# A carried block's cast and low placed further behind its transfers, and two columns of an output product computed as a pair with two quads

## The chip, the cores and the metric

The kernel runs on one core of a Trainium2 chip. The metric is the device time of one execution in microseconds (us), as a median of several. The engines are named as in the profile: PE is TensorE's matmuls and PEld its weight loads, DVE is VectorE, ACT is ScalarE, POOL is GpSimd, SP is SyncE, which here only issues transfers.

## The reference

One layer with a sequence of 256 tokens and a width of 2048, all in fp32: a feed-forward part, a mixer and a second feed-forward part, each with a norm before and after it and added to what came in.

```python
f = _swiglu(_rmsnorm(h, ln_ffn1_pre[l]), ffn1_gate[l], ffn1_up[l], ffn1_down[l])
h = h + MACARON_WEIGHT * _rmsnorm(f, ln_ffn1_post[l])
mx = _hybrid_mixer(_rmsnorm(h, ln_mix_pre[l]), w_in[l], ..., w_out[l])
h = h + _rmsnorm(mx, ln_mix_post[l])
f = _swiglu(_rmsnorm(h, ln_ffn2_pre[l]), ffn2_gate[l], ffn2_up[l], ffn2_down[l])
h = h + MACARON_WEIGHT * _rmsnorm(f, ln_ffn2_post[l])
```

`_swiglu` is `(silu(x @ w_gate) * (x @ w_up)) @ w_down` with 5632 inner columns. The mixer computes a recurrent branch and a pooling branch, gates and adds them to `m`, and returns `m @ w_out`, with `w_out` 2048 x 2048. The change touches the two feed-forward parts and this last product.

## The kernel before, in words

**Products.** Each fp32 operand is split in two: `wH` is the weight rounded by a cast on ACT (L151), `wL` the rest, a subtraction on DVE (L152). One product is three matmuls, wH·xH, wL·xH and wH·xL (`mm3`, L175 to L177), each over 512 weight columns. Weights come in pairs of two k rows by 512 columns: one transfer of 512 KB issued by SP (L137) into one of four `w32` buffers, one cast, one low, into one of five buffers each for `wH` and `wL`. A k row is multiplied with both halves of the tokens (128 each), so a pair takes 12 matmuls.

**Pairs of columns and quads.** `seven` (L321) does two column blocks together, f then l: first f's pairs, then l's. A few k pairs are done as quads instead (`quad`, L358): two k rows of both columns at once, with 7 products for 8, in the manner of Strassen. A quad needs sums of weights on DVE (`t13` L374, the halves of `t24` L378 and L382), casts (L389) and lows (L390) of weights and sums, and sums of activations made ahead (`sums`, L254: L265 to L277 on DVE, high parts on ACT L310, lows L314). It takes 21 matmuls in place of 24 and collects into the banks p1, p5, p6 and p7 ("ms" in the profile) besides the columns' own banks ("mm"). Behind the last quad comes `merge` (L406): ACT copies p1 into a buffer `u` (L411), DVE adds p6, p7, p5 and p5, then f's two own banks (L414); then f's result is evaluated. Adding l's banks (`total`, L423) comes at the end.

**Feed-forward.** Its 5632 inner columns are eleven blocks of 512, b = 0 to 10, each a gate (f) and an up column block (l). Blocks 2 to 10 use `seven` with three quads (`NG`, `SPOTS`), so ten pairs and three quads, 183 matmuls. The third quad comes behind the second pair of l's part; then three pairs follow, beside which the merge runs. There are four "mm" banks, two of f and two of l, so the next block's first matmul needs a bank that the merge has read.

**The carried block.** A block's result is multiplied, transposed 32 by 32 on DVE (L589) and then carried into the next block (`carry_at`, L591): 8 us after that block's start POOL issues sixteen transfers `x<-T` (L601) that complete the transpose. For each token half h follow the cast on ACT (`high`, L613) at `CARRY[h]` behind the transfers' issue and the low on DVE (`low`, L617) 2 us after it. The result is a part of `hT`, which only the down product reads. That product (`post`, L726) has 44 k rows and two column pairs, with seven and eight quads; the last 16 k rows of its last column are done by token halves (`by_half`, `TRAIL`), so that the norm and the next transposes of the first half run beside the second.

**The output product** `m @ w_out` is the same `post` with 16 k rows: four column blocks, each by `gemm_tok` (L179) with eight pairs, the last by halves.

**What sets the order.** The order of instructions on PE, ACT and DVE is written out ahead by a plan of times: `put` (L128) queues matmuls, each with its time (0.2265 us per matmul), `at` (L101) places an event at a time of this plan, and `slot` (L106) gives the planned time at which a weight buffer comes free. `run` (L112) writes the instructions in that order; nothing reorders them on the chip. POOL's and SP's instructions follow in the order in which they were written.

Of the kernel before, what the change touches and what calls it, by code (L numbers as in the profile page):

```python
# [22 lines left out]
NKD = D // P  # L23
NKF = DFF // P
# [17 lines left out]
TRAIL = 16  # L42
# [1 line left out]
TURNS = [[4.2, 5.3, 6.4, 7.5], [5.3, 6.0, 6.7, 7.4]]  # L44
WARM = 12
TB = 4
NQ = {False: 7, True: 8}
QUADS = {False: ((8, 12), (0, 3, 5, 7, 9)), True: ((2, 4, 6, 8, 10, 12), (1, 3))}
FAST = range(2, 11)
CARRY = (10, 13)  # L50
NG, SPOTS = 3, ((2, 4), (1,))

ROWS = [("ln_mix_pre", 16), ("ln_ffn2_pre", 16), ("mu", 26), ("w0", 8), ("a0", 8),
# [4 lines left out]
class Block:  # L58
# [259 lines left out]
                                                  else (third, fourth))):  # L318
            s.at(when + 1.7 * i, fn)

    def seven(s, wf, cf, wl, cl, at, KT, T, sm, n, spots, ev_first, ev_last, trail=False,  # L321
              one_end=False):


# [79 lines left out]
        u = []  # L404

        def merge():  # L406
            m = s.clk

            def start():
                u.extend(s.tmp("u") for _ in range(4))  # L410
                nc.scalar.copy(u[0], bank["p1"])  # L411

            def add(o, b, i):
                V.tensor_tensor(out=u[o], in0=bank[b], in1=u[i], op=ALU.add)  # L414
            s.at(m + 0.2, start)
            for j, a in enumerate(((1, "p6", 0), (2, "p7", 1), (1, "p5", 1), (3, "p5", 2),
                                   (1, "f0", 1), (3, "f1", 3))):
                s.at(m + 0.7 + 0.1 * j, lambda a=a: add(*a))
            s.at(m + 4, lambda: ev_first(0, u[1]))
            s.at(m + 4.6, lambda: ev_first(1, u[3]))  # L420

        def total(h):
            V.tensor_tensor(out=u[2 * h], in0=bank[f"l{h}"], in1=u[2 * h], op=ALU.add)  # L423
# [5 lines left out]
        def both():  # L429
            total(0)  # L430
            total(1)
            ev_last((u[0], u[2]))
        q = 0
        stop = KT - (TRAIL if trail else 0)
        for part, w, c0, b in ((0, wf, cf, "f"), (1, wl, cl, "l")):
            for i, k in enumerate(range(K0, stop if part else KT, 2)):
                pair(k, w, c0, b)
                if i in spots[part]:
                    quad(q)
                    q += 1  # L440
                    if q == n:
                        merge()
        if trail:
            s.by_half(wl, cl, stop, KT, s.clk, AHEAD[0],
                      lambda k, h: mul(f"l{h}", rows(k, h), ws[k]), keep, finish)
# [145 lines left out]
    def carry_at(s, T1, T, t):  # L591
# [28 lines left out]
        for h in range(2):  # L620
            s.at(t + CARRY[h], lambda h=h: high(h))
            s.at(t + CARRY[h] + 2, lambda h=h: low(h))

# [3 lines left out]
    def ffn(s, wg, wu, wd, uT, rs, gpost, resid, emit, reload, xs=None):  # L627
        nc = s.nc
        hT, sm = [], []
        at = s.T_at(uT)  # L630
        nb = NKF // 4

        st = {}

        def block(b):
            sig = [None, None]
            T1 = []

            def turned(h, src):
                if not T1:  # L640
                    T1.append(s.unit(p="T1"))
                s.turn(T1[0], h, src)

            def ev_g(h, ps):
                sig[h] = s.tmp("sg")
                nc.scalar.activation(out=sig[h], in_=ps, func=AF.Silu, scale=r[h])

            def ev_f(h, u):
                sig[h] = u
                nc.scalar.activation(out=u, in_=u, func=AF.Silu)  # L650

            def ev_l(o):
                for h in range(2):
                    nc.vector.tensor_tensor(out=o[h], in0=o[h], in1=sig[h], op=ALU.mult)
                for h in range(2):
                    turned(h, o[h])

            def ev_um(h, ps):
                nc.vector.scalar_tensor_tensor(out=sig[h], in0=ps, scalar=r[h], in1=sig[h],
                                               op0=ALU.mult, op1=ALU.mult)  # L660
                turned(h, sig[h])

            r = rs if b < 2 else [1.0, 1.0]
            if b > 0:
                s.carry_at(*st["T1"], s.clk + 8)
            st["T1"] = (T1, hT)
            if b == 0:
                s.gemm_tok(wg, 0, at, NKD, ev_g, lead=True, xs=xs)
                s.gemm_tok(wu, 0, at, NKD, ev_um, hold=True)
                while s.after:  # L670
                    s.after.pop(0)()
                st["rb"] = s.rtmp("rsb")
                s.spread(rs, st["rb"])
                return
            if b == 1:
                st["nT"], st["su"] = s.normed(uT, st["rb"], s.clk + 4), []
                s.sums(st["nT"], st["su"], s.clk + 16)
                s.sums(st["nT"], st["su"], s.clk + 27, nq=1)
            nT, su = st["nT"], st["su"]
            if b in FAST:  # L680
                s.seven(wg, b * 512, wu, b * 512, s.T_at(nT), NKD, nT, su, NG, SPOTS,
                        ev_f, ev_l, one_end=True)
                return
            x = at if b == 1 else s.T_at(nT)
            s.gemm_at(wg, b * 512, x, NKD, ev_g)
            s.gemm_at(wu, b * 512, x, NKD, ev_um)

        for b in range(nb):
            block(b)
        s.carry_at(*st["T1"], s.clk + 8)  # L690
        s.post(wd, s.T_at(hT), NKF, gpost, 0.5, resid, emit, reload, hT, sm)

    def spread(s, rs, out):

# [28 lines left out]
            s.at(t + 9.5 * i, lambda i=i: one(i))  # L723
        return nT

    def post(s, wd, at, KT, gpost, fac, resid, emit, reload, hT=None, sm=None):  # L726
        nc = s.nc
        gb = [s.unit(p="gb") for _ in range(2)]
        fg = [[s.unit(p="fg") for _ in range(2)] for _ in range(2)]
        ss = [s.small(4, "ss") for _ in range(2)]  # L730

        def cc_(u, c):
            return u[c // 2][:, (c % 2) * 512:(c % 2) * 512 + 512]

        part = [None, None]
        kf = 1.0 / (D * fac ** 2)

        late = 0.7 if hT is not None else 0.0

        def ev_of(c):  # L740
            def ev(h, ps):
                if h == 0 and c % 2 == 0:
                    nc.gpsimd.dma_start(out=gb[c // 2], in_=gpost[c * 512:c * 512 + 1024]
                                        .partition_broadcast(P))
                def scale():
                    nc.vector.tensor_tensor(out=cc_(fg[h], c), in0=ps, in1=cc_(gb, c),
                                            op=ALU.mult)
                s.sumsq(ps, ss[h][:, c:c + 1])
                if c < 3:
                    scale()  # L750
                if c == 2 and h == 0:
                    reload()
                if c == 2:
                    p = s.small(1, "rt", bufs=2)
                    nc.vector.tensor_reduce(out=p, in_=ss[h][:, :3], axis=AX.X, op=ALU.add)
                    part[h] = s.small(1, "rp", bufs=2)
                    nc.vector.tensor_scalar(out=part[h], in0=p, scalar1=kf,
                                            scalar2=NORM_EPS / fac ** 2, op0=ALU.mult,
                                            op1=ALU.add)
                if c == 3:  # L760
                    end = s.now + late
                    r = s.small(1, "rs", bufs=8)
                    s.at(end + 0.9, lambda: (norm(h, r), scale()))
                    for q in range(4):
                        s.at(end + 1.7 + 0.7 * q, lambda q=q: out(h, q, r, end))

            def norm(h, r):
                r2 = s.small(1, "rt2", bufs=2)
                nc.vector.tensor_scalar(out=r2, in0=ss[h][:, 3:4], scalar1=kf,
                                        scalar2=part[h], op0=ALU.mult, op1=ALU.add)  # L770
                nc.gpsimd.tensor_tensor(out=r, in0=r2, in1=s.mhalf[:, :1], op=ALU.pow)

            def out(h, q, r, end):
                o = cc_(fg[h], q)
                nc.vector.scalar_tensor_tensor(out=o, in0=o, scalar=r, in1=resid(h, q),  # L775
                                               op0=ALU.mult, op1=ALU.add)
                emit(h, q, o, end + TURNS[h][q])
            return ev
        if hT is not None:
            own = {}  # L780
            for t in (3, 24, 40, 76):
                s.sums(hT, sm, s.clk + t, own)
            for c in (0, 2):
                ev = ev_of(c)
                s.seven(wd, c * 512, wd, c * 512 + 512, at, KT, hT, sm, NQ[c == 2], QUADS[c == 2],
                        ev, ev_of(c + 1), c == 2)
            return
        for c in range(4):
            s.gemm_tok(wd, c * 512, at, KT, ev_of(c), trail=(c == 3))

    def next_pre(s, gT):
        uT = s.new_T(4)
# [93 lines left out]
    def mixer(s, prm, uT, rs, resid, emit, gpost, reload):  # L886
        nc = s.nc
        w_in = prm["w_in"]
        at = s.T_at(uT)
# [108 lines left out]
        mT = s.new_T(4)  # L998
# [52 lines left out]
            pass  # L1051
        for c in range(2, 4):
            s.gemm_tok(prm["w_proj_a"], c * 512, at_a, NKW, ev_pa(c))
        s.post(prm["w_out"], s.T_at(mT), NKD, gpost, 1.0, resid, emit, reload)

    def pool_window(s, g, win, at, w_in, mxT):
        nc = s.nc
# [490 lines left out]
```

## Time and profile before

| what | value |
|---|---|
| runs, us | 2066.42, 2072.79, 2066.91; median 2066.91 |
| profiled execution, us | 2066.3 |
| its span, us | 2064.6 |
| its mean granted clock of TensorE | 0.998 |
| instructions | 30104 |
| bytes moved by DMA | 418.63 MB, mean 203 GB/s |
| weight transfers of the output product | 32 of 512 KB |

The span is that of the traced instructions; the execution's own time has 1.7 us more around it. In the views a row of a timeline has the start, the length, the engine, the source line, the operation, and in brackets how long the engine was idle before it and what ended that. A row "A <- B: total, times, longest" of the waits says how long A's engine stood for B. Rows of windows have busy times by engine, then the granted clock, the DMA share and GB/s.

### The profile page before, as it was taken

To read this page: it belongs to the slowest core of one execution; us is meant where nothing else is said; L and a number is where in the kernel's file an instruction comes from. 1 tells how busy PE (TensorE), PEld (TensorE's weight loads), DVE (VectorE), ACT (ScalarE), POOL (GpSimd) and SP (SyncE) were. 2 spreads that over 40 slices of the span, in tenths; PEclk is the share of its full clock that TensorE was granted. 3 is DMA by queue.
4 is the path that set the end of the run, shared out by engine and by line. 5 is a ranking of instruction groups with operands and counts; after the bars stand their busy time and mean duration, and the time that the engine had idled before them with its cause. 6 is when DMAs were issued, how large, how long until landed. Compare 5 with 4: busy or idle time off the path is not lost. (4 is left out here: it accounts for less than half of the span.)

```text
span 2064.6 us, 30104 instructions
## 1 busy us (share of the span) xinstructions
PE 2037.2 (99%) x10841; PEld 1709.5 (83%) x10841; DVE 1725.6 (84%) x2278; ACT 1131.1 (55%) x1502; POOL 248.9 (12%) x513
## 2 busy tenths in 40 slices
PE   9999999999999999999999999999999999999998
PEld 7888878878888799999888788888887778788886
DVE  6999999989998865799688666579999999889986
ACT  7555555555555574474465444465555555555553
POOL 0121111211000000000110110011211112110000
PEclk9999999999999999999999999999999999999999
DMA  7666666756667666656456566666666666666674
GB/s 259 192 203 216 214 223 196 221 187 212 205 214 260 217 189 185 179 159 199 130 157 190 162 245 188 200 215 193 200 218 213 218 200 211 198 203 214 214 258 150
DMA packets 238079, 418.63 MB, mean 203 GB/s; under 512 B 21471, under 2 KB 57449, under 8 KB 237929
## 3 DMA queue, kind: packets, MB, share of 16 engines
q1 hardware_dynamic: 220489, 384.70, 59.8%
q0 software_dynamic: 17152, 31.48, 4.6%
q8 instruction: 85, 1.39, 0.3%
q10 hardware_dynamic: 288, 0.52, 0.1%
q14 instruction: 65, 0.53, 0.1%
HBM read 396.69 MB, written 8.39 MB: 196 GB/s over the span
## 5 line engine op out<-in xcount | busy, mean ns | idle before, releaser
L152 DVE TENSOR_TENSOR wL<-w,wH 128x1024 fp32r<-128x1024 f32 (+2 forms) x557 | 661.0, 1206 | 233.3 <-ACT wH L151 228.4
L175 PE MATMUL mm<-wH,xH 128*128 128x512 f32 x1956 | 766.9, 393 | 10.5 <-DVE u L414 7.5
L151 ACT CAST wH<-w 128x1024 fp32r<-128x1024 f32 (+2 forms) x557 | 569.9, 1041 | 357.9 <-PE mm L177 171.8
L176 PE MATMUL mm<-wL,xH 128*128 128x512 f32 x1956 | 763.0, 390 | 2.2 <-DVE wL L152 2.2
L177 PE MATMUL mm<-wH,xL 128*128 128x512 f32 x1956 | 762.8, 390 | 0.7 <-DVE xL L579 0.7
L175 PEld LDWEIGHTS mm<-wH,xH 128*128 128x128 f32 x1956 | 367.5, 188 | 93.0 <-issue 12.7
L176 PEld LDWEIGHTS mm<-wL,xH 128*128 128x128 f32 x1956 | 367.7, 188 | 78.7 <-DVE wL L152 4.3
L177 PEld LDWEIGHTS mm<-wH,xL 128*128 128x128 f32 x1956 | 367.6, 188 | 78.6 <-DVE xL L579 1.5
L389 ACT CAST wH<-t 128x1024 fp32r<-128x1024 f32 x168 | 177.0, 1053 | 280.5 <-DVE t L382 198.1
L601 POOL DMA_DIRECT2D x<-T x352 | 172.8, 499 | 754.5 <-issue 484.9
L390 DVE TENSOR_TENSOR wL<-t,wH 128x1024 fp32r<-128x1024 f32 x168 | 203.2, 1220 | 9.2 <-ACT wH L389 5.9
L390 DVE TENSOR_TENSOR wL<-w,wH 128x1024 fp32r<-128x1024 f32 (+1 forms) x168 | 159.2, 948 | 1.3 <-ACT wH L389 1.3
L543 PE MATMUL mc<-xH,wH 128*128 128x256 f32 x560 | 159.5, 285 | 0.0
L543 PE MATMUL mc<-xL,wH 128*128 128x256 f32 x560 | 158.4, 283 | 0.0
L543 PE MATMUL mc<-xH,wL 128*128 128x256 f32 x560 | 158.3, 283 | 0.0
L389 ACT CAST wH<-w 128x1024 fp32r<-128x1024 f32 (+1 forms) x168 | 137.7, 832 | 25.8 <-DMA w<-in_ffn_down_dram 17.4
L374 DVE TENSOR_TENSOR t<-w,w 128x1024 f32<-128x1024 f32 x84 | 102.4, 1219 | 6.7 <-issue 4.0
L543 PEld LDWEIGHTS mc<-xH,wH 128*128 128x128 f32 x560 | 106.0, 189 | 1.1
L543 PEld LDWEIGHTS mc<-xH,wL 128*128 128x128 f32 x560 | 106.0, 189 | 0.2
L543 PEld LDWEIGHTS mc<-xL,wH 128*128 128x128 f32 x560 | 106.0, 189 | 0.1
L176 PE MATMUL ms<-wL,sH 128*128 128x512 f32 x168 | 65.6, 390 | 0.0
L175 PE MATMUL ms<-wH,sH 128*128 128x512 f32 x168 | 65.5, 390 | 0.0
(308 smaller groups left out, 2154.7 us busy)
## 6 DMA issues: line engine op xcount, KB each, us to landing
w<-in_w_in_dram SPq DMA_DIRECT2D x128, 512.0 KB
w<-in_ffn_up_dram SPq DMA_DIRECT2D x122, 512.0 KB
w<-in_ffn_gate_dram SPq DMA_DIRECT2D x120, 512.0 KB
w<-in_ffn_down_dram SPq DMA_DIRECT2D x116, 512.0 KB
w<-in_ffn_down_dram SPq DMA_DIRECT2D x120, 256.0 KB
w<-in_ffn_gate_dram SPq DMA_DIRECT2D x112, 256.0 KB
w<-in_ffn_up_dram SPq DMA_DIRECT2D x108, 256.0 KB
w<-in_w_out_dram SPq DMA_DIRECT2D x32, 512.0 KB
```

The costliest lines, as they stand in the source:

```text
L151: s.nc.scalar.copy(vH, v)
L152: s.nc.vector.tensor_tensor(out=vL, in0=v, in1=vH.bitcast(F32), op=ALU.subtract)
L175: nc.tensor.matmul(ps, aH, bH, start=start, stop=False)
L176: nc.tensor.matmul(ps, aH, bL, start=False, stop=False)
L177: nc.tensor.matmul(ps, aL, bH, start=False, stop=stop)
L374: V.tensor_tensor(out=v["t13"], in0=v["a"], in1=v["b0"].to_broadcast([P, 2, 512]), op=ALU.subtract)
L389: nc.scalar.copy(H, v[n_])
L390: V.tensor_tensor(out=L, in0=v[n_], in1=H.bitcast(F32), op=ALU.subtract)
L543: s.nc.tensor.matmul(o, lh, rh, start=one and n == 0, stop=k == KT - 1 and n == 2, skip_group_check=True)
L601: nc.gpsimd.dma_start(out=x[0][q * 32:q * 32 + 32, i], in_=src[i * 32:i * 32 + 32, q])
```

## The change

It has two parts. `CARRY` goes from (10, 13) to (18, 21), so that the carried block's casts and lows stand 8 us further on in the plan; its transfers keep their place. And `post` takes a plan of its column blocks: for the down products it holds the numbers from before (`DOWN`), for the output product (`OUT`) column 0 stays as it was, columns 1 and 2 go through `seven` as a pair with two quads, one after the fifth pair of column 1, one after the first pair of column 2, and column 3 stays by halves. The sums of the activations for these quads are planned at the start. `merge` is split so that f's own banks can be added at the end of f's part, which no plan here uses, and `late`, which moves the last column's norm and transposes in the plan, is 0.7 for the output product as well, where it was 0. Lines of the kernel move by one to ten (L617 becomes L626, L414 becomes L415).

```diff
-NQ = {False: 7, True: 8}
-QUADS = {False: ((8, 12), (0, 3, 5, 7, 9)), True: ((2, 4, 6, 8, 10, 12), (1, 3))}
+DOWN = ((0, 7, ((8, 12), (0, 3, 5, 7, 9)), 0),
+        (2, 8, ((2, 4, 6, 8, 10, 12), (1, 3)), TRAIL))
+OUT = ((0, 0, (), 0), (1, 2, ((4,), (0,)), 0), (3, 0, (), TRAIL))
...
-CARRY = (10, 13)
+CARRY = (18, 21)
...
         def merge():
...
-            for j, a in enumerate(((1, "p6", 0), (2, "p7", 1), (1, "p5", 1), (3, "p5", 2),
-                                   (1, "f0", 1), (3, "f1", 3))):
+            for j, a in enumerate(((1, "p6", 0), (2, "p7", 1), (1, "p5", 1), (3, "p5", 2))):
                 s.at(m + 0.7 + 0.1 * j, lambda a=a: add(*a))
-            s.at(m + 4, lambda: ev_first(0, u[1]))
-            s.at(m + 4.6, lambda: ev_first(1, u[3]))
+
+            def first(m):
+                s.at(m, lambda: add(1, "f0", 1))
+                s.at(m + 0.1, lambda: add(3, "f1", 3))
+                s.at(m + 2.9, lambda: ev_first(0, u[1]))
+                s.at(m + 3.5, lambda: ev_first(1, u[3]))
+            return first
...
-        q = 0
-        stop = KT - (TRAIL if trail else 0)
+        q, first = 0, None
+        stop = KT - trail
...
                     if q == n:
-                        merge()
+                        first = merge()
+                        if part:
+                            first(s.clk + 1.1)
+            if not part and first:
+                first(s.clk + 0.3)
...
-        s.post(wd, s.T_at(hT), NKF, gpost, 0.5, resid, emit, reload, hT, sm)
+        s.post(wd, s.T_at(hT), NKF, gpost, 0.5, resid, emit, reload, hT, sm,
+               (((3, 2), (24, 2), (40, 2), (76, 2)), {}, DOWN))
...
-        late = 0.7 if hT is not None else 0.0
+        late = 0.7
...
+        times, own, plan = plan
+        for t, nq in times:
+            s.sums(hT, sm, s.clk + t, own, nq)
+        for c, n, spots, trail in plan:
+            if not n:
+                s.gemm_tok(wd, c * 512, at, KT, ev_of(c), trail=(c == 3))
+                continue
+            s.seven(wd, c * 512, wd, c * 512 + 512, at, KT, hT, sm, n, spots, ev_of(c),
+                    ev_of(c + 1), trail)
...
-        s.post(prm["w_out"], s.T_at(mT), NKD, gpost, 1.0, resid, emit, reload)
+        s.post(prm["w_out"], s.T_at(mT), NKD, gpost, 1.0, resid, emit, reload, mT, [],
+               (((0, 2),), None, OUT))
```

On ACT, in the sixth block (b = 5) of the first feed-forward, around the third quad, the order before was this; `x` is the carried block, `w` are weights, `t` sums of weights:

```order
L613 CAST xH_2383<-x_1215_2276 128x4x128
L151 CAST wH_2388<-w_1242_2386 128x1024
L151 CAST wH_2400<-w_1245_2398 128x1024
L389 CAST wH_2417<-w_1248_2408 128x1024
L613 CAST xH_2383<-x_1215_2276 128x4x128
L389 CAST wH_2429<-w_1249_2409 128x512
L389 CAST wH_2441<-t_1250_2414 128x1024
L389 CAST wH_2457<-t_1251_2415 128x1024
```

The carry's two casts (xH) stand before the third quad's casts (w of 2408 and 2409, t) and between them. Now the same place reads:

```order
L390 CAST wH_2413<-w_1246_2404 128x1024
L390 CAST wH_2424<-w_1247_2405 128x512
L390 CAST wH_2435<-t_1248_2410 128x1024
L390 CAST wH_2451<-t_1249_2411 128x1024
L622 CAST xH_2467<-x_1215_2276 128x4x128
L152 CAST wH_2473<-w_1260_2471 128x1024
L622 CAST xH_2467<-x_1215_2276 128x4x128
L152 CAST wH_2486<-w_1263_2484 128x1024
```

Both casts stand behind the quad's last one, with one weight pair's cast between them.

On DVE at the same place the order before, from the carry's first low (xL) on to the pairs' lows behind the quad:

```order
L617 TENSOR_TENSOR xL_2384<-x_1215_2276,xH_2383 128x4x128
L374 TENSOR_TENSOR t_1250_2414<-w_1248_2408,w_1249_2409 128x1024
L390 TENSOR_TENSOR wL_2418<-w_1248_2408,wH_2417 128x1024
L378 TENSOR_TENSOR t_1251_2415<-w_1248_2408,t_1250_2414 128x512
L390 TENSOR_TENSOR wL_2430<-w_1249_2409,wH_2429 128x512
L382 TENSOR_TENSOR t_1251_2415<-w_1249_2409,t_1251_2415 128x512
L617 TENSOR_TENSOR xL_2384<-x_1215_2276,xH_2383 128x4x128
L390 TENSOR_TENSOR wL_2442<-t_1250_2414,wH_2441 128x1024
L390 TENSOR_TENSOR wL_2458<-t_1251_2415,wH_2457 128x1024
L152 TENSOR_TENSOR wL_2476<-w_1260_2473,wH_2475 128x1024
```

And now, from the third quad's last two lows to the first add of the merge (u):

```order
L391 TENSOR_TENSOR wL_2436<-t_1248_2410,wH_2435 128x1024
L391 TENSOR_TENSOR wL_2452<-t_1249_2411,wH_2451 128x1024
L626 TENSOR_TENSOR xL_2468<-x_1215_2276,xH_2467 128x4x128
L153 TENSOR_TENSOR wL_2474<-w_1260_2471,wH_2473 128x1024
L153 TENSOR_TENSOR wL_2487<-w_1263_2484,wH_2486 128x1024
L153 TENSOR_TENSOR wL_2496<-w_1266_2493,wH_2495 128x1024
L626 TENSOR_TENSOR xL_2468<-x_1215_2276,xH_2467 128x4x128
L153 TENSOR_TENSOR wL_2509<-w_1269_2506,wH_2508 128x1024
L153 TENSOR_TENSOR wL_2521<-w_1272_2518,wH_2520 128x1024
L415 TENSOR_TENSOR u_2537<-ms_2343,u_2536 128x512
```

One of the carry's lows stands behind the quad's now, the other behind three pairs' lows, with two more pairs' lows between it and the merge.

On DVE in the output product, behind the evaluation of column 0 (fg), the order before held only lows of weight pairs:

```order
L746 TENSOR_TENSOR fg_12476<-mm_12481,gb_12472 128x512
L152 TENSOR_TENSOR wL_12710<-w_3086_12707,wH_12709 128x1024
L152 TENSOR_TENSOR wL_12716<-w_3089_12713,wH_12715 128x1024
L152 TENSOR_TENSOR wL_12746<-w_3092_12743,wH_12745 128x1024
L152 TENSOR_TENSOR wL_12752<-w_3095_12749,wH_12751 128x1024
```

Now the low of column 1's fifth pair is followed by the activations' sums (sx, sf, sL) and the first quad's operands (t and the lows from w and, behind these rows, from t):

```order
L756 TENSOR_TENSOR fg_12476<-mm_12481,gb_12472 128x512
L153 TENSOR_TENSOR wL_12666<-w_3144_12663,wH_12665 128x1024
L266 TENSOR_TENSOR sx_12669<-xH_6716,xL_6717 128x1024
L273 SCALAR_TENSOR_TENSOR sf_12685<-sx_12669 128x256
L275 SCALAR_TENSOR_TENSOR sf_12685<-sf_12685,sx_12669 128x256
L277 TENSOR_TENSOR sf_12685<-sx_12669 128x256
L278 TENSOR_TENSOR sf_12685<-sx_12669,sf_12685 128x256
L375 TENSOR_TENSOR t_3153_12696<-w_3151_12690,w_3152_12691 128x1024
L391 TENSOR_TENSOR wL_12700<-w_3151_12690,wH_12699 128x1024
L379 TENSOR_TENSOR t_3154_12697<-w_3151_12690,t_3153_12696 128x512
L315 TENSOR_TENSOR sL_12717<-sf_12685,sH_12716 128x1024
L391 TENSOR_TENSOR wL_12721<-w_3152_12691,wH_12720 128x512
```

The lows of the first four pairs stand ahead of these rows, that of the sixth behind them, and two pairs' lows per column are gone.

More of the change, by code (lines that the diff above doesn't have):

```diff
@@ L319, in sums, with seven @@
             s.at(when + 1.7 * i, fn)
[L321 removed]
+    def seven(s, wf, cf, wl, cl, at, KT, T, sm, n, spots, ev_first, ev_last, trail=0,
               one_end=False):
@@ L724, in normed, with post @@
         return nT
-    def post(s, wd, at, KT, gpost, fac, resid, emit, reload, hT=None, sm=None):
+    def post(s, wd, at, KT, gpost, fac, resid, emit, reload, hT, sm, plan):
         nc = s.nc
@@ L778, in ev_of @@
             return ev
[L779 to L789, printed above, removed]
+        times, own, plan = plan
[7 more added lines that the diff above has]
+                    ev_of(c + 1), trail)
     def next_pre(s, gT):
```

## The prediction

> **What bounds the kernel now.** I read the page's totals first, then the waits of TensorE, then busy times cut at the end of each feed-forward block's third quad, and last the timelines around the places that these point to. The totals:
>
> ```profile
> PE 2037.2 (99%) x10841; PEld 1709.5 (83%) x10841; DVE 1725.6 (84%) x2278; ACT 1131.1 (55%) x1502; POOL 248.9 (12%) x513
> ```
>
> TensorE is busy for 99% of the span, so only two things can pay: fewer matmuls, or the few places where it waits or runs slowly. Its waits (total us, times, longest us):
>
> ```profile
> PE mm L175 <- DVE u L414: 7.5, 9, 1.9
> PE mm L175 <- ACT wH L151: 2.8, 2, 1.8
> PE mm L176 <- DVE wL L152: 2.2, 3, 0.8
> PE tr L571 <- DVE fg L775: 0.6, 1, 0.6
> ```
>
> The largest is nine waits for the merge's adds. Where nothing waits, its matmuls start 0.22 us apart, here in the output product:
>
> ```profile
> 1298.22 0.39 PE L176 MATMUL mm<-wL,xH 128*128 128x512 f32 x1
> 1298.44 0.39 PE L177 MATMUL mm<-wH,xL 128*128 128x512 f32 x1
> ```
>
> Cut from one third quad's end to the next (first column the length; then busy us of PE, PEld, DVE, ACT and POOL; then the granted clock), a block shows how much time it loses. Here are the first clean block and the last two of the first feed-forward with the sum of its eight, then the worst block of the second with that one's sum:
>
> ```profile
> 132.19:173.67 41.48, 41.48 (x185) 34.35 (x184) 39.12 (x46) 23.53 (x27) 7.83 (x16) 1.00 0.67 215
> ...
> 384.31:429.39 45.08, 42.46 (x184) 34.05 (x183) 38.65 (x46) 23.01 (x27) 7.86 (x16) 1.00 0.63 198
> 429.39:473.22 43.83, 41.88 (x184) 34.19 (x183) 39.40 (x46) 23.37 (x27) 7.84 (x16) 1.00 0.65 205
> sum 341.03, PE 334.85 PEld 273.58 DVE 313.06 ACT 186.90 POOL 62.72; mean PE 41.86 PEld 34.20 DVE 39.13 ACT 23.36 POOL 7.84
> ```
>
> ```profile
> 1728.52:1774.42 45.90, 44.01 (x185) 35.30 (x184) 40.26 (x47) 24.46 (x28) 7.85 (x16) 0.96 0.64 198
> ...
> sum 341.30, PE 336.18 PEld 274.89 DVE 314.18 ACT 187.67 POOL 62.71; mean PE 42.02 PEld 34.36 DVE 39.27 ACT 23.46 POOL 7.84
> ```
>
> A block without a loss lasts 41.48 us, for ten pairs of 12 matmuls and three quads of 21, so 41.48 / 183 = 0.227 each. Eight would be 331.84, so the first feed-forward loses 341.03 − 331.84 = 9.19 us here and the second 341.30 − 331.84 = 9.46. Two kinds of place make this up. The first is the ninth block of each, where the carried block's cast (L613) waits for its sixteen transfers, and ACT, DVE and TensorE stop behind it in turn:
>
> ```profile
> 404.23 5.39 POOL L601 DMA_DIRECT2D x<-T  x11 [36.99 <-ACT wH L151]
> 416.32 0.62 ACT L613 CAST xH<-x 128x512 fp32r<-128x512 f32 x1 [4.46 <-DMA x<-T]
> 417.92 2.36 DVE L152 TENSOR_TENSOR wL<-w,wH 128x1024 fp32r<-128x1024 f32 x2 [4.80 <-ACT wH L151]
> 417.94 0.50 PE L175 MATMUL mm<-wH,xH 128*128 128x512 f32 x1 [1.81 <-ACT wH L151]
> 419.20 0.50 PE L176 MATMUL mm<-wL,xH 128*128 128x512 f32 x1 [0.76 <-DVE wL L152]
> ```
>
> ```profile
> 1761.43 0.50 PE L175 MATMUL mm<-wH,xH 128*128 128x512 f32 x1 [1.00 <-ACT wH L151]
> 1762.69 0.71 PE L176 MATMUL mm<-wL,xH 128*128 128x512 f32 x1 [0.76 <-DVE wL L152]
> 1763.00:1766.40 3.40, 3.40 (x9) 2.66 (x9) 3.40 (x4) 2.09 (x4) 0.00 (x0) 0.53 0.73 226
> ```
>
> The last of these rows is a stretch: behind the second stall the granted clock was 0.53 for 3.40 us, which costs 3.40 × 0.47 = 1.6 us more than the two idles.
>
> The second kind is the start of most blocks, whose first matmul needs a bank that the previous merge still reads. Here is one block on DVE, with ACT's last cast and TensorE's first matmul behind it:
>
> ```profile
> 245.53 2.36 DVE L152 TENSOR_TENSOR wL<-w,wH 128x1024 fp32r<-128x1024 f32 x2 [1.06 <-ACT wH L151]
> ...
> 252.48 0.68 DVE L617 TENSOR_TENSOR xL<-x,xH 128x512 fp32r<-128x512 f32 x1
> ...
> 261.53 1.22 DVE L152 TENSOR_TENSOR wL<-w,wH 128x1024 fp32r<-128x1024 f32 x1 [1.55 <-ACT wH L151]
> 262.67 2.73 DVE L414 TENSOR_TENSOR u<-ms,u 128x512 f32<-128x512 f32 x4
> 265.32 1.28 DVE L414 TENSOR_TENSOR u<-mm,u 128x512 f32<-128x512 f32 x2
> ```
>
> ```profile
> 260.45 1.05 ACT L151 CAST wH<-w 128x1024 fp32r<-128x1024 f32 x1 [1.89 <-PE mm L177]
> ```
>
> ```profile
> 266.15 0.47 PE L175 MATMUL mm<-wH,xH 128*128 128x512 f32 x1 [0.33 <-DVE u L414]
> ```
>
> DVE is idle twice per block: 1.06 us behind the carry's cast (245.53) and 1.55 before the last low (261.53). With a mean of 39.1 busy and these two it needs 39.1 + 1.06 + 1.55 = 41.7 us, more than the 41.48 that TensorE takes. So DVE falls behind from block to block, until each merge's adds end after the time at which TensorE is ready. Without the carry's idle it would need 40.7 and keep up.
>
> **Part 1: the carried block's casts and lows 8 us later.** Nothing is added or taken away, on any engine; four instructions per block move on ACT and DVE. The sixteen transfers stay where they are, ahead of everything else on POOL's queue, and SP's queue is not passed. They are issued and land so:
>
> ```profile
> 232.64 7.83 POOL L601 DMA_DIRECT2D x<-T  x16 [34.22 <-issue]
> ```
>
> ```profile
> DMA to landing us min/median/max: 1.6/3.4/6.3
> ```
>
> The last lands at most 7.83 + 6.3 = 14.1 us after the first issue, at 246.8 here. The casts now stand behind the third quad's last cast, whose low follows 252.48, so nothing waits for a transfer. In the ninth block ACT was at the cast by 416.32 − 4.46 = 411.86 and had its data at 416.32; 8 us later, near 420, it waits for nothing. The two idles of 4.46 and 4.80 us go, with TensorE's behind them and the slow clock.
>
> For the other blocks: what moves on DVE are two lows of 0.68 us (252.48). One stands right behind the third quad's lows now, the other three weight lows further on. The carry's idle (1.06 at 245.53) is gone, and of the two lows only one stands ahead of the low that frees the last pair's buffer, where it was two. So DVE reaches that low 1.06 + 0.68 = 1.74 us earlier, the weight transfer behind it starts earlier by as much, and the cast at 260.45, which closes the chain to the adds, as well. The adds then end near 266.6 − 1.74 = 264.9. TensorE lost 0.33 at 266.15 as the row has it, and the block's excess is about one us at most, so 1.74 covers it. Late next is the last cast, paced by its transfer; its slack is then about one us.
>
> What ACT has queued behind the moved casts are the next weight pairs' casts. Those have 0.62 us each to give, since ACT is busy for 23.4 us of a block. The carried block is used in the down product alone; for the last one, whose carry runs inside that product, the lows come 31 us after its start, while its last k rows are reached after 13 pairs of 12 matmuls, 13 × 12 × 0.227 = 35 us, and two quads. So nothing waits for it either. Value: between 0 and 9.19 + 9.46 = 18.65 us. I take all of it but 1.5 us, since the clean block above shows that TensorE runs at 41.48 while DVE keeps up. Two stalls of the same origin lie outside the windows, at the starts of the first down product and in the second:
>
> ```profile
> 482.30 0.47 PE L175 MATMUL mm<-wH,xH 128*128 128x512 f32 x1 [0.74 <-DVE u L414]
> 1854.56 0.50 PE L176 MATMUL mm<-wL,xH 128*128 128x512 f32 x1 [0.72 <-DVE wL L152]
> ```
>
> They are worth 0.74 + 0.72 = 1.5 us.
>
> A page of the Trainium skill ("TensorE: Matmul & The Clock Gate", section "HAM oscillation — how this bites in real kernels") says that TensorE's clock falls back after idle gaps of more than about 3.4 us. The stall at 1761 had idles of 1.00 and 0.76 and the clock fell to 0.53 behind it, so the trace does not agree here. By the rule a stall that remains costs its length alone; by the trace it can cost 1.6 us on top, and I use the trace's price below.
>
> **Part 2: the output product's columns 1 and 2 as a pair.** Two quads each do 7 products of 3 matmuls where 8 stood: 2 × 3 = 6 matmuls fewer. At 0.227 that is 1.36 us less. What DVE gets for it, with the rows for its free time in these columns (44 us) and for each width of operation:
>
> ```profile
> sum 44.00, DVE 22.83; mean DVE 11.41
> ```
>
> ```profile
> L374 DVE TENSOR_TENSOR t<-w,w 128x1024 f32<-128x1024 f32 x84 | 102.4, 1219 | 6.7 <-issue 4.0
> L414 DVE TENSOR_TENSOR u<-ms,u 128x512 f32<-128x512 f32 x88 | 58.6, 687 | 1.5
> ```
>
> The sums of the activations: two operations of 1.22 and four over 128x256, which I estimate from the two rows' widths at 0.687 − (1.219 − 0.687) / 2 = 0.42, 4.1 in all. Each quad: four operations of 1.22 and three of 0.68, 6.9, in place of two pair lows, 2.4: +4.5, twice 9.0. Merge and totals: eight adds of 0.69, 5.5. Together +18.6, against 44 − 22.8 = 21.2 us of idle time. It fits. TensorE reaches the first quad after five pairs of 12 × 0.227 = 2.72, 13.6 us into column 1, and its last operand 3.4 us later, at 17.0. DVE has ahead of that low 4.1 + 6.9 and, for pairs, about three of 1.22, near 15 us: some 2 us to spare. If that cover goes, TensorE stands for the difference once. The merge has five pairs behind it, 13.6 us, for 4 adds, one copy and the first half's evaluation. The transfers move the same bytes. The last column's tail starts its transposes 0.7 us later in the order: at best 0, at worst the 0.6 us of the row for tr L571 above, from the first feed-forward's tail that has this lateness already. I take 0, since the tail's transposes stand behind matmuls that run anyway.
>
> **Sum** on the profiled execution, 2066.3 us: 2066.3 − 18.65 − 1.5 − 1.36 + 1.5 (left over) = 2046.3. The median of the runs shown is 2066.91, 0.6 above the profiled one, so 2047 in round numbers. Its own range: 2044.5 (nothing left over: 2044.8 + 0.6 = 2045.4, and one us of scatter) to 2050.
>
> **Rivals.**
>
> *R1, the merges stay late.* If the last cast's time is set by the transfer itself and not by the buffer that DVE frees, DVE's earlier arrival only lengthens its idle at 261.53. For it: ACT waited 1.89 before 260.45, behind the issue of that very transfer. Against: the block at 132.19 runs clean with its transfers at 215 GB/s, the one at 429.39 loses 2.35 us at 205, so more than the transfers' rate decides. Then only the ninth blocks' losses go, at most 45.08 − 41.48 = 3.60 and 45.90 − 41.48 = 4.42, with 0.72 and 1.36: 10.1 us, 2056.8. If part of those two stays, some 2058 to 2061.
>
> *R2, slower: the lows now stand right before the merge.* The two lows moved from ahead of the third quad to behind it, 1.37 us closer to the adds. If the cast ahead of the last low does not come earlier, and DVE is no longer idle before it (1.55 at 261.53), the adds end up to 1.37 us later, and each of 18 blocks starts that much later: 24.7 us. It decides from the point where that idle falls under 1.37. With the 10.1 of R1 gained, 2066.3 + 24.7 − 10.1 + 0.6 = 2081.5. Against it: DVE's work up to the adds is the same and its idle of 1.06 is gone.
>
> *R3, the pair does not pay.* In its columns DVE would be busy for 22.8 + 18.6 = 41.4 us of 44 − 1.36 = 42.6. If the first quad's operands come late by more than the 2 us to spare, TensorE stalls once or twice, 1 to 2 us each, with up to 1.6 for the clock: +2 to +6 us on the forecast, 2049 to 2053. Beside this: the Trainium skill ("Perfetto Trace Analysis", section "Identifying the Most-Contended Engine") judges TensorE by its weight loads' busy share, not its matmuls', and by that (83% against DVE's 84%) DVE is the most contended engine, to which the pair adds. The trace speaks for TensorE: its starts at 1298 follow each other by 0.22 with no gap.
>
> **Chances.** Forecast 0.66, R1 0.20, R3 0.10, R2 0.04. About 0.3% (6.2 us) is what a measurement of this kernel tells from no change; all of the forecast and R3 and 0.14 of R1 lie under 2060.7: faster 0.90, same 0.06 (R1's upper part), slower 0.04. The range from 2044 to 2058 holds the forecast, R3 and the middle of R1.
>
> **What would show it.** Right: no wait of ACT for x<-T in the feed-forward blocks; no wait of TensorE for the adds from 224 to 490 and from 1560 to 1740 but a few tenths; blocks of 41.5 to 41.7 from third quad to third quad; granted clock 1.00 at the place of 1763; six matmuls fewer and no wait of TensorE in the output product's columns 1 and 2. R1: the waits for the adds stay, with a longer idle of DVE before the last low. R2: they grow, with that idle gone. R3: a wait for a quad's low or sum, or for the pair's merge. Wrong altogether: blocks that stay at 42.5 with no wait of DVE for ACT at the carry.

## The result, and the profile after

| | kernel before | changed kernel |
|---|---|---|
| median, us | 2066.85 | 2044.34 |
| range of four runs, us | 2066.42 to 2072.79 | 2043.64 to 2044.87 |
| profiled execution, us | 2066.3 | 2044.42 |
| its span, us | 2064.6 | 2042.7 |

The ratio is 0.9884, with a 95% interval from 0.9866 to 0.9902 (the two medians alone give 0.9891). The change is 22.5 us faster by the medians; forecast were 19.9 (2066.9 to 2047.0). A second set of runs gave 2044.31 and 0.9888 (0.9873 to 0.9903).

First the totals of the changed kernel and all that TensorE waits for in it:

```profile
PE 2030.0 (99%) x10835; PEld 1710.9 (84%) x10835; DVE 1749.1 (86%) x2302; ACT 1137.5 (56%) x1508; POOL 245.8 (12%) x513
```

```profile
PE warm L477 <- POOL ident masks.py:199: 1.7, 1, 1.7
PE tr L580 <- DVE fg L785: 0.6, 1, 0.6
PE tr L580 <- DMA x<-in_x_dram: 0.5, 1, 0.5
PE pSa L1386 <- ACT us L1381: 0.4, 1, 0.4
PE mm L176 <- DVE u L415: 0.3, 1, 0.3
```

Of the nine waits for the merge's adds (7.5 us) one of 0.3 is left; those for a weight's cast and low (wH, wL) are gone. The totals have six matmuls fewer. ACT's waits for the carry's transfers, which in the kernel before were these, are gone too:

```profile
ACT xH L613 <- DMA x<-T: 30.1, 20, 4.5
```

Cut again from one third quad's end to the next, these are blocks of the first feed-forward (the third, the seventh and the last of eight, then their sum), and the second's worst and sum:

```profile
215.89:257.37 41.48, 41.48 (x184) 34.35 (x183) 39.68 (x46) 23.69 (x27) 7.81 (x16) 1.00 0.69 216
...
381.81:423.29 41.48, 41.48 (x184) 34.35 (x183) 39.69 (x46) 23.58 (x27) 7.83 (x16) 1.00 0.69 215
423.29:465.38 42.09, 41.81 (x185) 34.19 (x183) 39.55 (x46) 23.39 (x27) 7.81 (x16) 1.00 0.67 214
sum 332.45, PE 332.17 PEld 274.62 DVE 317.15 ACT 189.05 POOL 62.51; mean PE 41.52 PEld 34.33 DVE 39.64 ACT 23.63 POOL 7.81
```

```profile
1588.75:1630.37 41.62, 41.62 (x184) 34.19 (x183) 39.48 (x46) 23.44 (x27) 7.82 (x16) 1.00 0.67 215
...
sum 331.98, PE 331.98 PEld 274.62 DVE 317.26 ACT 189.02 POOL 62.53; mean PE 41.50 PEld 34.33 DVE 39.66 ACT 23.63 POOL 7.82
```

Each block but two lasts the 41.48 us of the one clean block quoted before; the ninth of the first feed-forward, 45.08 then, is among them. The eight blocks of each feed-forward went from 341.03 to 332.45 and from 341.30 to 331.98, so 8.58 + 9.32 = 17.90 us of the profile's 21.9 are here. The granted clock is 1.00 in all of them. Here is the same block on DVE as shown before, from the third quad's last lows on:

```profile
252.74 0.68 DVE L626 TENSOR_TENSOR xL<-x,xH 128x512 fp32r<-128x512 f32 x1
253.94 1.23 DVE L153 TENSOR_TENSOR wL<-w,wH 128x1024 fp32r<-128x1024 f32 x1 [0.51 <-ACT wH L152]
255.41 2.36 DVE L153 TENSOR_TENSOR wL<-w,wH 128x1024 fp32r<-128x1024 f32 x2 [0.24 <-ACT wH L152]
257.69 0.68 DVE L626 TENSOR_TENSOR xL<-x,xH 128x512 fp32r<-128x512 f32 x1
258.29 1.22 DVE L153 TENSOR_TENSOR wL<-w,wH 128x1024 fp32r<-128x1024 f32 x1
259.94 1.22 DVE L153 TENSOR_TENSOR wL<-w,wH 128x1024 fp32r<-128x1024 f32 x1 [0.43 <-ACT wH L152]
261.08 2.73 DVE L415 TENSOR_TENSOR u<-ms,u 128x512 f32<-128x512 f32 x4
263.74 1.28 DVE L415 TENSOR_TENSOR u<-mm,u 128x512 f32<-128x512 f32 x2
```

The carry's two lows stand where the order put them, and in these rows no idle time of DVE longer than 0.51 is left. The first of the two last adds, which frees the next block's bank, ends at 263.74 + 0.68 = 264.42, 7.05 us after the third quad's end (257.37, the edge of the first window row above). TensorE needs the bank 36 matmuls after that end, 36 x 0.2267 = 8.16 us. So 1.1 us of slack is left in this block. In the kernel before, the same add ended at 265.32 + 0.68 = 266.00, 8.50 us after that block's third quad (257.50), so later than TensorE needed it.

### The profile page after: what moved, and what is told of

The parts are those of the page before. It is cut to its first block, busy times and chain, and to the rows that moved or that the text cites. A ratio compares the mean times of both kernels' runs of the same rounds, so it can differ in the third digit from the quotient of the medians.

```text
span 2042.7 us, 30133 instructions
## 1 busy us (share of the span) xinstructions
PE 2030.0 (99%) x10835; PEld 1710.9 (84%) x10835; DVE 1749.1 (86%) x2302; ACT 1137.5 (56%) x1508; POOL 245.8 (12%) x513
## 4 chain that ended last, share of the span: by engine, by line
PE 96%; DVE 1%; issue 1%; DMA 0%; ACT 0%; POOL 0%; POOLq 0%; DVEq 0%; ACTq 0%
PE mm L176 24%; PE mm L177 24%; PE mm L178 24%; PE mc L552 10%; PE ms L177 4%; PE ms L178 4%; PE ms L176 4%; PE tr L580 1%; DVE wL L153 0%; PE pA L1278 0%; DVE u L415 0%; DMA x<-in_x_dram 0%; PE pSa L1386 0%; DMA w<-in_ffn_down_dram 0%; PE pU L1374 0%
## 5 line engine op out<-in xcount | busy, mean ns | idle before, releaser
L177 PE MATMUL mm<-wL,xH 128*128 128x512 f32 x1944 | 757.4, 390 | 0.0
L177 PEld LDWEIGHTS mm<-wL,xH 128*128 128x128 f32 x1944 | 365.5, 188 | 74.6 <-DVE wL L153 0.5
L390 ACT CAST wH<-t 128x1024 fp32r<-128x1024 f32 x172 | 181.3, 1054 | 285.0 <-DVE t L383 160.1
L391 DVE TENSOR_TENSOR wL<-t,wH 128x1024 fp32r<-128x1024 f32 x172 | 210.0, 1223 | 9.4 <-ACT wH L390 4.9
L391 DVE TENSOR_TENSOR wL<-w,wH 128x1024 fp32r<-128x1024 f32 (+1 forms) x172 | 163.5, 951 | 1.3 <-ACT wH L390 1.3
L177 PE MATMUL ms<-wL,sH 128*128 128x512 f32 x174 | 67.8, 389 | 0.0
L178 PE MATMUL ms<-wH,sL 128*128 128x512 f32 x174 | 67.7, 389 | 0.0
```

What stands on the lines that cost most here:

```text
L177: nc.tensor.matmul(ps, aH, bL, start=False, stop=False)
L178: nc.tensor.matmul(ps, aL, bH, start=False, stop=stop)
L390: nc.scalar.copy(H, v[n_])
L391: V.tensor_tensor(out=L, in0=v[n_], in1=H.bitcast(F32), op=ALU.subtract)
```

## The experiments

Two theories of the block-start waits were to be told apart. The prediction's: the carry's cast waits for its transfers, DVE is idle behind it, and with that idle time DVE has more to do per block than TensorE. The rival: the lows' place decides, since fewer of them stand ahead of the last pair's low. Then each part alone, the prediction's slower rival, and one size.

**The carried block alone.** The kernel before with this edit:

```diff
-CARRY = (10, 13)
+CARRY = (18, 21)
```

> The carried block's casts and lows 8 us later, the output product as before. If the two parts of the change are independent and the output product's pair is worth its 6 matmuls (1.36 us), this stands 1.4 us above the whole change: 2045.8 us against 2044.3, with feed-forward blocks of 41.48 us. If the pair hides or adds something of its own, the distance is another: below 1 or above 3 us.

Measured: 2046.29 us (2045.57 to 2047.42), ratio 0.9909 (0.9894 to 0.9923), 2.0 above the whole change by the medians, though not in one set with it; the eight blocks sum to 332.41 and 331.97. In its own set it is 19.7 us under the kernel before (2065.96), so this part carries nearly all of the gain.

**The output product's pair alone.** The changed kernel with `CARRY` back:

```diff
-CARRY = (18, 21)
+CARRY = (10, 13)
```

> The output product's pair with two quads, the carried block's casts and lows where they were. Theory: 6 matmuls fewer and no new stall, 1.4 us under the kernel before, 2065.4 us, with the feed-forward blocks' losses as before (9.2 and 9.5 us over eight blocks each). Rival (the pair does not pay): 2066.8 us or more, with waits of TensorE for a quad's operand or for the pair's merge.

Measured: 2065.95 us (2063.50 to 2069.48, ten runs), against 2065.96 for the kernel before in the same set (fourteen runs from 2063.91 to 2071.28); ratio 1.0001 (0.9992 to 1.0011). The time cannot tell 1.4 us from nothing here, since both kernels scatter by several us from run to run. In the trace of this run the eight blocks of each feed-forward lose 9.95 and 10.11 us (341.79 and 341.95 against 331.84), 1.4 more than in the trace of the kernel before, as much as the pair is worth. The trace can tell, in another stretch: the one from the last quad of the first down product's first column pair to the third quad of the second feed-forward's first fast block, which holds the whole mixer, lasts so in the kernel before (first) and in the changed one:

```profile
sum 890.86, PE 888.99 PEld 768.38 DVE 677.28 ACT 484.58 POOL 81.97; mean PE 888.99 PEld 768.38 DVE 677.28 ACT 484.58 POOL 81.97
```

```profile
sum 889.45, PE 888.14 PEld 767.06 DVE 694.05 ACT 488.75 POOL 79.42; mean PE 888.14 PEld 767.06 DVE 694.05 ACT 488.75 POOL 79.42
```

By the same cut it is 890.86, 890.90, 890.80 and 891.25 in the four kernels without the pair (before, the carried block alone, no wait, late lows), and 889.45, 889.98, 889.97, 889.69 and 889.85 in the five with two quads, one trace each. The means differ by 890.95 − 889.79 = 1.16 us. The pair pays, by a little under its 1.36.

**No wait, in the old order.** The kernel before, in which the carry's casts and lows read the block as it is before its transfers; it leaves out what the transfers bring, so its result is not the layer's:

```diff
         def by_k(h):
-            return x[0][:, :, h].rearrange("p i k c -> p k i c")
+            return T1[0].rearrange("p (j h k c) -> p h k j c", j=4, h=2, k=4)[:, h]
```

> The kernel before with one thing changed: the carried block's casts and lows read the block as it is before its transfers (T1) and not what the transfers bring, so they wait for nothing; the transfers still run, and the result of the down products is another than the reference's. The order on every engine is that of before. Theory (DVE's idle time behind the waiting cast makes the merges late): all block-start waits go, not only those of the ninth blocks; blocks of 41.5 us, 2046 us. Rival (the lows' place decides, since two lows less stand ahead of the last pair's low): only the ninth blocks' own losses go, 8 us, 2058 us.

Measured: 2045.30 us (2045.06 to 2046.88), ratio 0.9905 (0.9890 to 0.9920). Sums of the eight blocks, first and second feed-forward:

```profile
sum 332.14, PE 332.14 PEld 274.64 DVE 315.86 ACT 189.59 POOL 62.51; mean PE 41.52 PEld 34.33 DVE 39.48 ACT 23.70 POOL 7.81
```

```profile
sum 332.03, PE 332.03 PEld 274.62 DVE 316.10 ACT 189.11 POOL 62.52; mean PE 41.50 PEld 34.33 DVE 39.51 ACT 23.64 POOL 7.82
```

With nothing moved and only the wait taken away, all block-start losses go, not the ninth blocks' alone. The rival's 2058 is out by 13 us. The wait is enough to explain the whole loss. In the block shown before, the last adds now start here:

```profile
263.04 1.28 DVE L414 TENSOR_TENSOR u<-mm,u 128x512 f32<-128x512 f32 x2
```

TensorE's bank is free at 263.04 + 0.68 = 263.72, 7.15 us after the third quad (256.57, an edge of the windows), where it was 8.50 with the wait and the same order.

**The lows late, the casts where they were.** The kernel before with this edit, so that DVE has the changed kernel's order and ACT the old one:

```diff
-            s.at(t + CARRY[h] + 2, lambda h=h: low(h))
+            s.at(t + CARRY[h] + 10, lambda h=h: low(h))
```

> The kernel before with only the carried block's lows 8 us later; its casts, which wait for the transfers, stay where they were. The order on DVE is that of the changed kernel, the order on ACT that of before. Theory (idle time behind the waiting cast): the ninth blocks' losses stay and most block-start waits too; DVE gains at most one low of 0.68 us per block ahead of the merge: 2060 to 2066 us. Rival (the lows' place decides): the block-start waits go and the ninth blocks' stalls stay, 2066.8 - 18.65 + 8.0 = 2056 us.

Measured: 2058.15 us (2057.53 to 2060.27), ratio 0.9965 (0.9950 to 0.9979), between the two expectations. Here are ACT's waits for the transfers in the first feed-forward (14.8 us, 10 times in the kernel before), TensorE's for the adds in the whole kernel, then each feed-forward's ninth block and sum:

```profile
ACT xH L613 <- DMA x<-T: 15.7, 10, 4.8
```

```profile
PE mm L175 <- DVE u L414: 2.1, 6, 0.5
```

```profile
382.89:429.43 46.54, 43.69 (x185) 35.42 (x184) 40.08 (x46) 23.78 (x28) 7.85 (x16) 0.96 0.63 196
...
sum 339.30, PE 335.55 PEld 275.19 DVE 315.67 ACT 189.11 POOL 62.61; mean PE 41.94 PEld 34.40 DVE 39.46 ACT 23.64 POOL 7.83
```

```profile
1723.72:1768.39 44.67, 42.07 (x185) 34.25 (x183) 38.60 (x45) 22.86 (x27) 7.84 (x16) 1.00 0.64 199
...
sum 338.38, PE 334.37 PEld 273.72 DVE 315.28 ACT 188.88 POOL 62.59; mean PE 41.80 PEld 34.22 DVE 39.41 ACT 23.61 POOL 7.82
```

The ninth blocks lose 5.06 and 3.19 us, 8.25 together (8.02 before): their loss belongs to the waiting cast. The other blocks lose (339.30 − 331.84) + (338.38 − 331.84) − 8.25 = 5.75, where it was 18.65 − 8.02 = 10.63. The kernel with the pair alone, whose lows are in the old place, loses 10.54 there. So while the casts wait, the place of the lows is worth about half of the block-start losses. That one low less ahead of the merge eases the same shortage of time on DVE is the likely reason, but no run shows it by itself. Taking the wait away does all of it, moving the lows half.

**Four us in place of eight.** The changed kernel with this edit:

```diff
-CARRY = (18, 21)
+CARRY = (14, 17)
```

> The changed kernel with the carried block's casts and lows 4 us later than before and not 8; they stand among the third quad's. Theory (a cast that waits for transfers is what makes the merges late): the waits of 1 to 2 us are gone and a few tenths of the 4.46 us wait are left in the ninth block, so nearly all of the gain: 2044.3 to 2047 us. Rival (the lows' place beside the merge): both lows stand ahead of the third quad's last one, as much DVE work ahead of the merge's last pair as before, so about half of the gain: 2052 to 2056 us.

Measured: 2043.90 us (2043.26 to 2045.56), ratio 0.9888 (0.9873 to 0.9903), the same as the whole change (2044.31 in this set). The eight blocks sum to 332.20 and 331.84. Between 4 and 8 us the exact place does not matter, since the casts wait for nothing in either. Of the two lows one stands ahead of the third quad's last low and one right behind it, so this is not quite the old place that the rival prices at half of the gain; the kernel without the wait has the old place, and there too the place costs nothing that can be measured.

**The lows directly before the merge's adds.** The changed kernel with this edit, which moves the casts on as well, among the last weight pairs' casts:

```diff
-CARRY = (18, 21)
+CARRY = (23.4, 23.45)
```

> The changed kernel with the carried block's two lows moved on until they stand directly before the merge's adds. The prediction's slower rival says that the adds then end up to 1.37 us later. In the changed kernel they end 7.05 us after the third quad and the next block needs the bank at 8.16, 1.1 us of slack: if all of the 1.37 arrives, each of 18 blocks stands about 0.3 us, 5 us in all: 2049.5 us. Theory: the last pair's low is paced by a transfer into a buffer that DVE frees, DVE gets there earlier by the two lows no longer ahead, so the adds move by under 1.1 us and nothing waits: 2044.3 us.

Measured: 2053.60 us (2053.38 to 2054.58), ratio 0.9934 (0.9920 to 0.9949), 9.3 above the changed kernel, beyond both expectations. Its DVE in the same block, TensorE's waits, and the sum of the first feed-forward:

```profile
254.37 3.73 DVE L153 TENSOR_TENSOR wL<-w,wH 128x1024 fp32r<-128x1024 f32 x3 [0.85 <-ACT wH L152]
258.67 1.23 DVE L153 TENSOR_TENSOR wL<-w,wH 128x1024 fp32r<-128x1024 f32 x1 [0.57 <-ACT wH L152]
260.74 1.23 DVE L153 TENSOR_TENSOR wL<-w,wH 128x1024 fp32r<-128x1024 f32 x1 [0.84 <-ACT wH L152]
261.88 1.29 DVE L626 TENSOR_TENSOR xL<-x,xH 128x512 fp32r<-128x512 f32 x2
263.08 2.73 DVE L415 TENSOR_TENSOR u<-ms,u 128x512 f32<-128x512 f32 x4
265.73 1.28 DVE L415 TENSOR_TENSOR u<-mm,u 128x512 f32<-128x512 f32 x2
```

```profile
PE mm L176 <- DVE u L415: 3.3, 8, 1.4
```

```profile
257.81:300.03 42.22, 41.78 (x184) 34.20 (x183) 39.58 (x46) 23.77 (x28) 7.83 (x16) 1.00 0.68 211
...
sum 336.97, PE 334.49 PEld 273.63 DVE 316.77 ACT 189.81 POOL 62.72; mean PE 41.81 PEld 34.20 DVE 39.60 ACT 23.73 POOL 7.84
```

The bank is free at 265.73 + 0.68 = 266.41, 8.60 us after the third quad's end (257.81), where TensorE is ready at 8.16. That is 1.55 us later than in the changed kernel: 1.2 for the two lows, and the last pair's low itself starts 0.36 later behind the quad (2.93 us, 2.57 there). DVE's earlier arrival did not bring the last cast forward, and the theory's half of that expectation fell. DVE now stands idle for 0.85 + 0.57 + 0.84 = 2.26 us between the quad and the adds, where the changed kernel has 0.51 + 0.24 + 0.43 = 1.18: there the lows fill part of the time for which DVE waits for casts, here they come behind the last such wait. Blocks last 42.1 on the mean (336.97 / 8) and not 41.48, twice the 0.3 us per block that the rival's arithmetic gave. Its mechanism is real. In the changed kernel both lows stand ahead of the last wait for a cast, and 1.1 us of slack are left.

**A third quad in the output product.** The changed kernel with:

```diff
-OUT = ((0, 0, (), 0), (1, 2, ((4,), (0,)), 0), (3, 0, (), TRAIL))
+OUT = ((0, 0, (), 0), (1, 3, ((2, 4), (0,)), 0), (3, 0, (), TRAIL))
...
-               (((0, 2),), None, OUT))
+               (((0, 2), (12, 1)), None, OUT))
```

> The changed kernel with three quads and not two in the output product's pair, and the activations' sums of one more k pair's half for it. TensorE has 3 matmuls less, 0.68 us. DVE gets 4.5 us for the quad and 2.5 for the sums on top of 38.2 busy of 44 us in these columns, 45.2, more than there is. Theory (DVE then bounds these columns): stalls of 1 to 3 us there, 2045 to 2047 us. Rival (there is room before and behind the columns): 2043.7 us with no stall.

Measured: 2050.86 us (2050.24 to 2053.99), ratio 0.9919 (0.9903 to 0.9936), 6.5 above the changed kernel. TensorE's largest two new stalls in the output product (they come just behind columns 1 and 2), the stretch after them, and the busy times of columns 1 and 2 in 44 us:

```profile
1329.78 0.51 PE L176 MATMUL mm<-wH,xH 128*128 128x512 f32 x1 [1.29 <-ACT wH L152]
1331.04 0.50 PE L177 MATMUL mm<-wL,xH 128*128 128x512 f32 x1 [0.75 <-DVE wL L153]
```

```profile
1331.40:1334.80 3.40, 3.40 (x10) 2.67 (x9) 2.99 (x3) 1.27 (x2) 0.00 (x0) 0.54 0.79 243
```

```profile
sum 44.00, PE 42.68 PEld 33.72 DVE 41.39 ACT 23.37 POOL 0.00; mean PE 21.34 PEld 16.86 DVE 20.70 ACT 11.69 POOL 0.00
```

With DVE busy for 41.4 of 44 us TensorE is busy for only 42.7 of them, and the stall behind the columns costs the clock as well. The theory's direction holds, its 1 to 3 us are too little. This profile is of the slowest of the four runs (2053.99), and part of its excess lies elsewhere: at 685 to 705, in the mixer, TensorE waits 1.1 and 0.8 us for a weight's cast and low and the clock is 0.91 to 0.92. With this placement DVE does not carry a third quad; other places for it were not tried.

## Why the prediction was right or wrong

**The mechanism was right; the step that failed is the size of the sum's terms.** On the profiled execution's scale the sum said 2046.3; measured was 2044.42, so the gain was put 1.9 us too small. Term by term:

| term | forecast, us | measured, us |
|---|---|---|
| losses in eight blocks of each feed-forward | −18.65 + 1.5 left over | −17.90 |
| stalls at the two down products | −1.5 | −2.25 |
| output product's pair | −1.36 | −1.41 |
| the rest (start, last tail) | 0 | −0.3 |

Two terms were mis-sized by 0.75 us each. The "left over" in the blocks was 0.75 and not 1.5. The stalls at the down products cost 2.25 and not 1.5: from the last block's third quad to the last quad of the down product's first column pair it took 110.52 us in the first feed-forward and 110.69 in the second, and 109.48 in both now, 1.04 + 1.21. The forecast took the idle times in the rows' brackets, 0.74 and 0.72, as the whole price. Around the first of them the kernel before has these two rows:

```profile
481.17 0.39 PE L177 MATMUL mm<-wH,xL 128*128 128x512 f32 x1
482.60 0.39 PE L176 MATMUL mm<-wL,xH 128*128 128x512 f32 x1
```

With the quoted row at 482.30 between them, the starts follow by 1.13 and 0.30 us in place of 0.227 each, so this one stall costs 0.98. The idle in brackets counts from the end of a matmul's 0.39 us, but without a stall the next starts 0.227 us after its start. A stall's price is the distance of the starts less 0.227.

On the scale of the medians the forecast also added the 0.6 us by which the median of before lay above its profiled execution; the changed kernel's median lies 0.08 under its own. So 2044.34 is just below the forecast's own range of 2044.5 to 2050 and just inside the wide one of 2044 to 2058; by the ratios the new time on the first median's scale is 0.9884 x 2066.91 = 2042.9 or 0.9888 x 2066.91 = 2043.8, under both. The lower ends took the profiled execution's losses as the most that there could be, though they differ between runs: the same blocks lose 18.65 us in that trace and 20.06 in that of the pair alone. The kernel before ran from 2063.9 to 2072.8 in all sets, the changed one from 2043.5 to 2044.9. Whether the wait for the transfers makes this scatter is not shown: the kernel with late lows, which still waits, spans 2.7 us in five runs, the one with three quads, which does not, 3.8 in four.

**The idle arithmetic** (39.1 + 1.06 + 1.55 against 41.48) has the right direction and too small a sum. The block from which the idle times are taken has DVE busy for 39.68 us and lasts 42.35, not 41.7; 39.1 is the mean over all blocks. In the kernel without the wait, with the same order, DVE is busy for 39.5 us and blocks take 41.48; the idle before the last low is still 1.25 there (before 259.25), and of the 1.06 at the carry 0.34 and 0.25 are left.

**The place of the lows.** The forecast had DVE reach that low 1.74 us earlier and the adds end near 264.9. They end at 263.74 + 1.28 = 265.02, with the quad 0.13 earlier. The cast that the forecast has at 260.45 is here:

```profile
258.86 1.05 ACT L152 CAST wH<-w 128x1024 fp32r<-128x1024 f32 x1 [1.58 <-DMA w<-in_ffn_gate_dram]
```

Behind the third quad it comes 1.49 us after in place of 2.95, so 1.46 earlier, and it now ends a wait for its weight transfer (the row of before names a matmul, L177, as what ended its wait of 1.89, which the forecast read as the transfer). The slack of "about one us" is 1.1. That the last cast always follows DVE is not so, as the kernel with the lows before the adds shows.

**R1** (merges stay late, 2056.8) is refuted: one such wait of 0.3 us is left. **R2** (slower) did not happen, but its mechanism is shown: 9.3 us when the lows stand directly before the adds. The forecast let it decide by the idle of 1.55 before the last low; what decided in the two kernels is whether the lows stand ahead of that idle or behind it. **R3** (the pair does not pay) is refuted by the trace; TensorE has no wait in these columns. Here are their busy times and, for the first quad, DVE's last two lows and TensorE's first matmul that needs the second of them:

```profile
sum 44.00, PE 43.97 PEld 36.10 DVE 38.23 ACT 24.10 POOL 0.00; mean PE 21.98 PEld 18.05 DVE 19.11 ACT 12.05 POOL 0.00
```

```profile
1286.75 2.51 DVE L391 TENSOR_TENSOR wL<-t,wH 128x1024 fp32r<-128x1024 f32 x2
```

```profile
1293.04 0.39 PE L177 MATMUL ms<-wL,sH 128*128 128x512 f32 x1
```

DVE is done at 1289.26, 3.8 us ahead; 2 were forecast. It is busy for 38.2 us of 44, not 41.4. Its added work was put too high (in the whole stretch of 889.45 us it is 694.05 − 677.28 = 16.8 us and not 18.6), and a part of that lies outside these columns. TensorE stands for DVE in these columns only with the third quad, at 41.4 of 44.

The Trainium skill ("Perfetto Trace Analysis", section "Identifying the Most-Contended Engine") says to judge TensorE by MFU, its share of the peak matmul rate, and by its weight loads' busy share, and to optimize the engine with the highest occupancy first. By the weight loads' share (83% before, DVE 84%) that is DVE, to which the pair adds work. The trace does not bear this out: TensorE has no gap in these columns and the stretch is 1.2 us shorter. The forecast left MFU out, and it was not worked out here.

## What to carry to other kernels

A short wait ahead of an engine that is nearly as busy as the bounding one (DVE, some 39 of 41.48 us) is not local: here it made that engine late for good, and showed far away, as a wait for the merge's adds. Before a step is moved behind its transfer, ask what then stands directly ahead of the next deadline: 8 us (or 4) further were free, 13 and 10 us, which put both lows directly before the adds, cost 9 of the 23 us gained. And price a stall of TensorE by the distance of the starts, not by the idle in brackets. To test such a cause, take the wait away with the order left alone, and change the order with the wait left in.

## What the runs showed of the hardware that was not expected

A stall of TensorE of about the same size sometimes cost its clock and sometimes not. The clock fell to about half behind idles of 1.00 and 0.76 us in the kernel before (0.53, at 1763) and of 1.29 and 0.75 in the kernel with three quads (0.54, above). It stayed at 1.00 in the kernel with late lows, behind longer idles:

```profile
1757.03 0.50 PE L175 MATMUL mm<-wH,xH 128*128 128x512 f32 x1 [1.84 <-ACT wH L151]
1758.28 0.50 PE L176 MATMUL mm<-wL,xH 128*128 128x512 f32 x1 [0.76 <-DVE wL L152]
```

```profile
1758.60:1762.00 3.40, 3.40 (x16) 2.81 (x15) 3.40 (x4) 2.36 (x4) 0.00 (x0) 1.00 0.76 225
```

So the length of the idles does not decide alone; what does was not tried. The price of such a stall in these traces is its length plus up to 3.40 x 0.47 = 1.6 us.
